# Layer borders of a seven-layer block: next layer's weights held early, its first products in a written order

## The chip, the cores and the metric

The kernel runs on one core of a Trainium2 chip. The metric is the device time of one execution in microseconds (us); several executions are timed and the median is given. The profile is of one further execution.

## The reference

One sequence of 512 tokens with 1024 features passes through two blocks. The first has a state-space mixer and a sliding-window attention, each between an RMS norm of its input and an RMS norm of its output:

```
for i in range(DEPTH):                       # mamba, then swa
    h = rmsnorm(x, pre_norm[i])
    y = mixer_i(h, ...)                      # ends in  o @ w_out
    x = x + rmsnorm(y, post_norm[i])
```

The second puts 16 meta tokens in front (528 tokens), and has a differential attention (da), a convolutional feed-forward (ffn0), a sparse attention with an index that picks keys (dsa), a second feed-forward (ffn1) and a final norm:

```
for i in range(DEPTH):                       # da, ffn0, dsa, ffn1
    h = h + attention_i(rms_norm(h, norm_i), w_in ...) @ w_o
    h = h + conv_ffn(rms_norm(h, ffn_norm[i]), w_up ...)   # u = h @ w_up first
```

A layer border is the stretch between the last product of one layer (`@ w_out`) and the first of the next (`h @ w_in`). At the borders mamba to swa and swa to da two norms lie in it, that of y and that of the new x.

## The kernel before

The features lie on the partitions, the tokens along the free axis; x is eight tiles `x[k]`. Every product is made in three terms to keep float32 accuracy: weights are split into `wH` and `wL`, the input into `hH` and `hL`, and for each of eight feature blocks k TensorE takes hH·wH, hH·wL and hL·wH (`gemm`, lines 353 to 368, and `project_v`, 785 to 805). `hH` comes from ScalarE (`high_of_x`, line 396), `hL` from VectorE (`low_of_x`, line 401). The norm's factor is not in h: it is multiplied into the product's result.

Weights arrive in chunks of eight 128x128 blocks: one load on SP's queue into `raw` (line 308), one ScalarE copy to `wH` (321), one VectorE subtraction to `wL` (323). `wH` and `wL` have a ring of four places each. `wget` has the chunk after the one asked for made as well.

A planner orders each engine's instructions when the program is built: of those that are ready by its own costs it takes the one that stands first in the program; a tile's place is given anew when its readers are done. The engines then run these fixed lists.

`norm_end` (line 459) makes the factor of the next norm: TensorE sums the squares over partitions (`token_sums`, 438), VectorE and GpSimd make the inverse root (`rsqrt`, 416 to 420: one GpSimd power, four small VectorE steps, the result is `rt`), TensorE spreads it over the partitions (`spread_rows`, 451 and 456), VectorE copies it to `rb` (468). `post_stats` does the same for the norm of y; its factor is `pr`.

`out_halves` (line 516 on) ends mamba and swa. For half 0 of the tokens, then half 1, it makes the eight output products of 12 matmuls, adds each to y (534) and collects squares (386 and 387). `post_update` then makes x = xs + y·factor (499, 500), `hH` and `hL` for one half. The order in the program is: half 0's products and factor; half 1's products; `post_update(0)`; two weight chunks (`W2 = 2`); half 1's factor; half 0's `post_norm` (squares, `norm_end`); `post_update(1)`; `post_norm(1)`. All four chunks of output weights lie in the ring.

swa begins with the keys (two products per half, then `rope`, lines 769 to 779) and the values (two tiles per half, line 797, brought out by ScalarE at 805 with `rt`). da begins with the values of five token tiles (16, 128, 128 in half 0; 128, 128 in half 1) for two groups of 256 columns. The other borders have no second norm: da and dsa end in `out_last`, ffn0 ends in its own loop, each with `norm_end(T)` as its last call, and ffn begins with `u = h @ w_up` in two column blocks per part. Results of these products go to five PSUM banks in turn (three `ps_g`, two `ps_s`).

Of the kernel before, what the change touches and what calls it, by code (L numbers as in the profile page):

```python
# [36 lines left out]
W1 = 0  # L37
W2 = 2
W3 = 0
# [176 lines left out]
class _Kernel:  # L216
# [225 lines left out]
    def spread_rows(self, src, T, half=None):  # L442
# [4 lines left out]
        for i, t0, tn in self.tok_tiles(T, half):  # L447
# [6 lines left out]
            if ps is None:  # L454
                ps, b0, n = self.ps("t"), t0, 0
# [4 lines left out]
    def norm_end(self, T, half=None):  # L460

        nc = self.nc
# [3 lines left out]
        self.rsqrt(self.rt[:, i0:i0 + n], v)  # L466
        for ps, t0, tn in self.spread_rows(self.rt, T, half):
            nc.vector.tensor_copy(self.rb[:, t0:t0 + tn], ps)

    def post_stats(self, half, acc, rg=None):  # L470
# [18 lines left out]
        return self.spread_rows(r, SEQ, half)[0][0]  # L489
# [17 lines left out]
    def post_norm(self, half, g_next, T_next):  # L507
# [3 lines left out]
        if g_next:  # L511
# [3 lines left out]
            self.norm_end(T_next, half)  # L515

    def out_halves(self, pool, H, L, ys, xs, g_post, g_next, T_next, acc, rg=None, part=True):
# [3 lines left out]
        n = len(H)  # L521

        for i in range(self.wi // 8, self.wi // 8 + n):
# [3 lines left out]
        ws = [self.wblocks(n) for m in range(KB)]  # L527
        rp = []
        for half in range(2):
            for m in range(KB):  # L530
                (ps, c0, cn), = self.gemm(ws[m], H, L, self.cuts(SEQ, half=half), spread=True)
                y = ys[m][:, c0:c0 + cn]
                if part:
                    nc.vector.tensor_tensor(y, ps, y, ALU.add)
                else:
                    nc.vector.tensor_copy(y, ps)
                self.square_in(y, m, c0, cn, nc.vector if m == KB - 1 else None, acc)
            if half == 1:
                for i in range(W1):
                    self.wchunk()  # L540
                self.post_update(0, rp[0], ys, xs, g_post, g_next, T_next)
                for i in range(W2):
                    self.wchunk()
            rp.append(self.post_stats(half, acc, rg))
        self.post_norm(0, g_next, T_next)
        for i in range(W3):
            self.wchunk()
        self.post_update(1, rp[1], ys, xs, g_post, g_next, T_next)
        self.post_norm(1, g_next, T_next)


    def mamba(self, g_next):
        nc, T = self.nc, SEQ
        tc = self.tc
        with ExitStack() as ctx:
# [210 lines left out]
            self.out_halves(op, yH[MF:], yL[MF:], yo, xo, "post0", g_next, SEQ, acc, rg)  # L766
# [17 lines left out]
    def project_v(self, vs, q, w, tiles, spread=False, meta=None):  # L784
# [3 lines left out]
        for i, t0, tn in tiles:  # L788
# [9 lines left out]
            qc = slice(256 * q, 256 * q + 256)  # L798
            if i == 0 and meta is not None:
                for r in range(2):  # L800
                    rv = lambda t: t.rearrange("p (b r n) -> p b r n", b=2, r=2)[:, :, r]
                    nc.scalar.activation(rv(meta[64 * r:64 * r + tn, qc]), rv(ps[:tn, :256]), AF.Copy,
                                         scale=self.rt[:tn, i:i + 1])
                continue
            nc.scalar.activation(vs[i][:tn, qc], ps[:tn, :256], AF.Copy, scale=self.rt[:tn, i:i + 1])
# [36 lines left out]

    def swa(self, g_next):
# [3 lines left out]
        with ExitStack() as ctx:  # L847
# [16 lines left out]
            kw = [self.wblocks(KB) for b in range(2)]  # L864
            vw = self.vweights()
            for half in range(2):
                cc = slice(256 * half, 256 * half + 256)
                nc.vector.tensor_tensor(C[:, cc], C[:, cc], self.rb[:, cc], ALU.mult)
                nc.vector.tensor_tensor(S[:, cc], S[:, cc], self.rb[:, cc], ALU.mult)
                for b in range(2):  # L870
                    self.rope(wp, self.gemm(kw[b], self.hH, self.hL, self.cuts(T, half=half), spread=True,
                                            late=True), C, S, kr[b])
                self.project_v(vs, 0, vw, self.tok_tiles(T, half), spread=True)
# [79 lines left out]
            if SF:  # L953
                for m in range(KB):
# [5 lines left out]
                            [x[:, META:] for x in self.x], "post1", g_next, T2, S, part=SF > 0)  # L960
# [129 lines left out]

    def da(self, g_next):
        nc, T = self.nc, T2
        with ExitStack() as ctx:
            cp = self.pool(ctx, "dc", 1, reuse_waits="tile")
# [23 lines left out]
            vw = [self.vweights() for q in range(2)]  # L1118
            for half in range(2):
                for q in range(2):  # L1120
                    self.project_v(vs, q, vw[q], self.tok_tiles(T, half), spread=True)
                for c0, cn in self.cuts(T, half=half):
                    nc.vector.tensor_tensor(C[:, c0:c0 + cn], C[:, c0:c0 + cn], self.rb[:, c0:c0 + cn], ALU.mult)
                    nc.vector.tensor_tensor(S[:, c0:c0 + cn], S[:, c0:c0 + cn], self.rb[:, c0:c0 + cn], ALU.mult)
# [143 lines left out]
    def out_last(self, H, L, g_next, lo=0):  # L1268
# [7 lines left out]
        if g_next:  # L1276
            self.norm_end(T)

# [213 lines left out]
    def ffn(self, i, g_next):  # L1492
# [6 lines left out]
        with ExitStack() as ctx:  # L1499
# [4 lines left out]
            for pi, part in enumerate(parts):  # L1504
                AH, AL = [], []
                for j in part:
                    cs = []
                    for s in range(2):
# [91 lines left out]
```

## Time and profile before

| | us |
|---|---|
| median of 3 runs | 2164.0 (2163.92 to 2164.73) |
| the profiled execution, its time | 2165.13 |
| its span, first to last instruction | 2162.7 |
| TensorE busy | 2076.2 (96%) |
| VectorE busy | 1488.3 (69%) |
| ScalarE busy | 1023.6 (47%) |
| GpSimd busy | 275.5 (13%) |
| granted TensorE clock, mean share of full | 0.981 |

The span is what the trace covers; the profiled execution's own time is 2.4 us more. Busy shares are means over all stages. In a timeline row the columns are start, duration, engine, line, operation, output and inputs, shape and count, and in brackets the idle time before it with what ended it.

### The profile page before, as it was taken

The numbers are of one execution on the slowest core, as the hardware profiler recorded it, in microseconds if no ns is written. First come the engines' busy times: TensorE is split into PE (matmuls) and PEld (weight loads), VectorE is DVE, ScalarE is ACT, GpSimd is POOL, SyncE is SP. The second block draws the span as 40 slices with busy tenths as digits, with TensorE's granted clock in tenths as the row PEclk, the third lists the DMA queues.
The fourth block names the chain that finished last, engine by engine and source line by source line (L and its number), as shares of the span: only waits on it lengthen the run. The fifth ranks groups of instructions, "written<-read, shape, count | busy, mean of one in ns | idle before, by whom it ended". The sixth has DMA issues, their size and how long they took to land. (4 is left out here: it accounts for less than half of the span.)

```text
span 2162.7 us, 37624 instructions
## 1 busy us (share of the span) xinstructions
PE 2076.2 (96%) x14812; PEld 1894.4 (88%) x14812; DVE 1488.3 (69%) x3215; ACT 1023.6 (47%) x1874; POOL 275.5 (13%) x433
## 2 busy tenths in 40 slices
PE   8999999989998899889999999989999999999998
PEld 6788888877777898879999999979888899999997
DVE  7786777787766666866763576489888667645653
ACT  6876555246675455644442343353455444423431
POOL 0211011141103222212000000210211020000001
PEclk9999999989999999989999999999999999999999
DMA  5333342413212222222332332311322222323221
GB/s 189 117 119 118 95 124 88 134 50 98 69 59 69 70 70 69 71 59 69 93 94 79 98 91 86 108 50 50 99 60 70 60 69 89 98 88 99 88 89 49
DMA packets 59567, 186.11 MB, mean 86 GB/s; under 512 B 8384, under 2 KB 12480, under 8 KB 59392
## 3 DMA queue, kind: packets, MB, share of 16 engines
q1 hardware_dynamic: 58240, 182.68, 28.2%
q8 instruction: 116, 1.90, 0.4%
q10 hardware_dynamic: 1152, 1.05, 0.1%
q14 instruction: 59, 0.48, 0.1%
HBM read 171.77 MB, written 2.23 MB: 80 GB/s over the span
## 5 line engine op out<-in xcount | busy, mean ns | idle before, releaser
L367 PE MATMUL ps_g<-hL,wH 128*128 128x256 f32 (+3 forms) x1912 | 606.7, 318 | 2.5 <-DVE hL L401 2.4
L367 PE MATMUL ps_g<-hH,wH 128*128 128x256 f32 (+3 forms) x1912 | 607.1, 318 | 1.4 <-ACT kr L775 1.1
L367 PE MATMUL ps_g<-hH,wL 128*128 128x256 f32 (+3 forms) x1912 | 606.5, 317 | 1.8 <-DVE wL L323 1.8
L321 ACT ACTIVATE wH<-raw 128x1024 fp32r<-128x1024 f32 x294 | 310.0, 1057 | 376.2 <-PE ps_g L367 217.1
L323 DVE TENSOR_TENSOR wL<-raw,wH 128x1024 fp32r<-128x1024 f32 x294 | 363.2, 1237 | 169.7 <-ACT wH L321 169.1
L367 PEld LDWEIGHTS ps_g<-hL,wH 128*128 128x128 f32 x1912 | 361.4, 189 | 26.9 <-DVE hL L401 3.9
L367 PEld LDWEIGHTS ps_g<-hH,wL 128*128 128x128 f32 x1912 | 362.3, 189 | 25.1 <-DVE wL L323 2.4
L367 PEld LDWEIGHTS ps_g<-hH,wH 128*128 128x128 f32 x1912 | 362.0, 189 | 24.1 <-ACT kr L775 1.2
L367 PE MATMUL ps_s<-hH,wH 128*128 128x256 f32 (+5 forms) x608 | 177.6, 292 | 8.0 <-ACT hH L396 8.0
L367 PE MATMUL ps_s<-hH,wL 128*128 128x256 f32 (+5 forms) x608 | 177.4, 292 | 0.6 <-DVE wL L323 0.6
L367 PE MATMUL ps_s<-hL,wH 128*128 128x256 f32 (+5 forms) x608 | 176.9, 294 | 0.7 <-DVE hL L401 0.6
L387 POOL TENSOR_TENSOR acc<-acc,sq 128x512 f32<-128x512 f32 (+3 forms) x62 | 78.1, 1260 | 555.5 <-ACT sq L386 554.1
L1519 DVE SCALAR_TENSOR_TENSOR c<-u,prm,c 128x528 f32<-128x528 f32 (+1 forms) x176 | 132.9, 755 | 1.6
L778 POOL TENSOR_TENSOR rt<-rt,S 128x272 f32<-128x272 f32 (+3 forms) x80 | 81.8, 1023 | 363.3 <-DVE rt L776 288.0
L367 PEld LDWEIGHTS ps_s<-hH,wH 128*128 128x128 f32 (+2 forms) x608 | 114.8, 189 | 10.4 <-ACT hH L396 9.1
L367 PE MATMUL ps_g<-aH,wH 128*128 128x256 f32 (+1 forms) x418 | 118.3, 283 | 0.3 <-ACT aH L810 0.2
L367 PEld LDWEIGHTS ps_s<-hL,wH 128*128 128x128 f32 (+2 forms) x608 | 114.3, 189 | 4.8 <-DVE hL L401 3.7
L367 PE MATMUL ps_g<-aL,wH 128*128 128x256 f32 (+1 forms) x418 | 118.2, 283 | 0.0
L367 PE MATMUL ps_g<-aH,wL 128*128 128x256 f32 (+1 forms) x418 | 118.0, 282 | 0.0
L367 PEld LDWEIGHTS ps_s<-hH,wL 128*128 128x128 f32 (+2 forms) x608 | 115.1, 189 | 3.3 <-DVE wL L323 1.4
L999 PE MATMUL ps_s<-k,q 128*128 128x272 f32 (+3 forms) x400 | 91.1, 323 | 13.6 <-DVE q L979 4.4
L810 ACT ACTIVATE aH<-sg 128x528 fp32r<-128x528 f32 (+1 forms) x44 | 28.1, 639 | 131.0 <-DVE sg L1524 131.0
(527 smaller groups left out, 4446.6 us busy)
## 6 DMA issues: line engine op xcount, KB each, us to landing
raw<-in_ws_dram SPq DMA_DIRECT2D x294, 512.0 KB, 3.7
k<-k SPq DMA_DIRECT2D x32, 264.0 KB, 3.1
m<-acs_d SPq DMA_DIRECT2D x32, 256.0 KB, 3.7
e<-eas_d SPq DMA_DIRECT2D x32, 96.0 KB, 2.8
x<-in_xT_dram SPq DMA_DIRECT2D x8, 256.0 KB, 4.9
xo<-in_xT_dram SPq DMA_DIRECT2D x8, 256.0 KB, 5.1
k<-k SPq DMA_DIRECT2D x4, 256.0 KB, 6.8
out_dram<-x SPq DMA_DIRECT2D x8, 128.0 KB, 1.7
```

The source lines that it names most:

```text
L321: nc.scalar.activation(H, self.raw, AF.Copy)
L323: nc.vector.tensor_tensor(L, self.raw, H.bitcast(F32), ALU.subtract)
L367: nc.tensor.matmul(ps[:M, :cn], w[k][a][:, :M], b[k][:, c0:c0 + cn], start=i == 0, stop=i == 3 * n - 1)
L387: (eng or nc.gpsimd).tensor_tensor(acc, acc, s[:, :cn], ALU.add)
L778: nc.gpsimd.tensor_tensor(t, t, S[:, cc], ALU.mult)
L810: nc.scalar.activation(H[:, cols], src, AF.Copy)
L999: nc.tensor.matmul(ps, q[:, r, t0:e], k[:, r, k0:k1], start=n == 0, stop=n == 1)
L1519: nc.vector.scalar_tensor_tensor(c[:, lo:], u[:, t + lo:t + T2], self.col(fw, 3 * b + t), c[:, lo:], ALU.mult, ALU.add)
```

## The change

- `out_halves`: of the four chunks of output weights two go to the ring and two to places of their own in the pool passed in. The chunks of the next layer follow in the ring: one after the fourth product of half 0 (if not yet made), one after the second and one after the fourth product of half 1. `W1`, `W2`, `W3` are gone.
- The factor of y's norm is made in two steps, `post_stats` and `post_spread`; the spread goes to the bank `ps_o`. `norm_end` is split into `norm_sums` and `norm_spread`.
- `front` is new. It takes up to four results ("banks"), and TensorE runs its part in the order written: for two banks at a time all products with hH, k by k; then `norm_sums`; then the products with hL for all banks, k by k; then `norm_spread`. Calls can be hung in after a given k.
- At the end of mamba and swa `front` is called for half 0 of the next layer. After the fourth k half 1's `post_stats` is hung in, after the twelfth (the fourth of the second pair) its `post_spread`. Then come `post_update(1)` and `post_norm(1)`, now without `norm_end`. The next layer calls `front` for half 1 (no calls hung in).
- `ahead(0)` gives what the next layer does with half 0's results (bringing out, tables, rope) a place in the program's order ahead of `post_update(1)`.
- da takes four of its six value products of half 0 in `front`, the two of the 16 tokens after it. Its pool `dc` is put on the right side of the memory.
- ffn0 and ffn1 take the first two parts' four column blocks in `front`; `norm_end` at the end of da and dsa is gone. The one at the end of ffn0 moves to the beginning of `dsa_index`, behind dsa's tables and memsets.

The diff, cut to its core:

```diff
-W1 = 0
-W2 = 2
-W3 = 0
...
     def norm_end(self, T, half=None):
+        self.norm_sums(T, half)
+        self.norm_spread(T, half)
...
+    def bank(self, w, c0, cn, M=P):
+        ps = self.ps(self.next_tag())[:M, :cn]
+        cc = slice(c0, c0 + cn)
+        return (ps, [[(w[k][a][:, :M], self.hH[k][:, cc]) for a in (0, 1)] for k in range(KB)],
+                [(w[k][0][:, :M], self.hL[k][:, cc]) for k in range(KB)])
...
+    def front(self, banks, T, half=None, hooks={}):
+        mm = self.nc.tensor.matmul
+        with self.tc.manual_schedule(engines={mybir.EngineType.PE}):
+            for b in range(0, len(banks), 2):
+                for k in range(KB):
+                    for ps, hs, ls in banks[b:b + 2]:
+                        for a, (w, h) in enumerate(hs[k]):
+                            mm(ps, w, h, start=k == 0 and a == 0, stop=False)
+                    hooks.get(KB * b // 2 + k, lambda: None)()
+            self.norm_sums(T, half)
+            for k in range(KB):
+                for ps, hs, ls in banks:
+                    w, h = ls[k]
+                    mm(ps, w, h, start=False, stop=k == KB - 1)
+            self.norm_spread(T, half)
+        return [b[0] for b in banks]
...
-        return self.spread_rows(r, SEQ, half)[0][0]
+        return r
+
+    def post_spread(self, r, half):
+        return self.spread_rows(r, SEQ, half, "o")[0][0]
...
-            self.norm_end(T_next, half)
...
+        c = self.wi // 8
+        for i in range(c, c + 4):
             if i >= self.wemit:
-                late = i - self.wi // 8 - 4
-                self.wchunk(*((pool, str(late)) if late >= 0 else ()))
+                self.wchunk(*((pool, str(i - c)) if i >= c + 2 else ()))
+        ws = [self.wblocks(4) for m in range(KB)]
...
+        for m in range(KB):
+            add(m, 0)
+            if m == 3 and self.wemit < c + 6:
+                self.wchunk()
+        rp = [self.post_spread(self.post_stats(0, acc, rg), 0)]
+        for m in range(KB):
+            add(m, 1)
+            if m in (1, 3):
+                self.wchunk()
+        second = []
+        self.post_update(0, rp[0], ys, xs, g_post, g_next, T_next)
         self.post_norm(0, g_next, T_next)
+        self.first = self.front(nxt(0), T_next, 0, {3: lambda: second.append(self.post_stats(1, acc, rg)),
+                                                    11: lambda: rp.append(self.post_spread(second[0], 1))})
+        self.prio = self.tc.cur_priority
         self.post_update(1, rp[1], ys, xs, g_post, g_next, T_next)
         self.post_norm(1, g_next, T_next)
+
+    def ahead(self, half):
+        tc = self.tc
+        return tc.high_priority(offset=tc.cur_priority - self.prio) if half == 0 else ExitStack()
...
+    def swa_first(self, half):
+        if half == 0:
+            self.fw = [self.wblocks(KB) for b in range(2)], self.vweights()
+        kw, vw = self.fw
+        return ([self.bank(w, 256 * half, 256) for w in kw] +
+                [self.bank_v(vw, t0, tn) for i, t0, tn in self.tok_tiles(SEQ, half)])
...
+                with self.ahead(half):
+                    ps = self.first if half == 0 else self.front(self.swa_first(1), T, 1)
+                    for (i, t0, tn), p in zip(tiles, ps[2:]):
+                        self.keep_v(vs, 0, i, tn, p)
...
+    def da_jobs(self, half):
+        t = self.tok_tiles(T2, half)[::-1]
+        return [(q, t) for ts in (t[:2], t[2:]) for q in range(2) for t in ts]
...
-            cp = self.pool(ctx, "dc", 1, reuse_waits="tile")
+            cp = self.pool(ctx, "dc", 1, reuse_waits="tile", side="right")
...
+                with self.ahead(half):
+                    ps = self.first if half == 0 else self.front(self.da_first(1), T, 1)
+                    for (q, (i, t0, tn)), p in zip(jobs, ps):
+                        self.keep_v(vs, q, i, tn, p)
+                    for q, t in jobs[4:]:
+                        self.project_v(vs, q, self.fw[q], [t], spread=True)
...
-        if g_next:
-            self.norm_end(T)
...
     def dsa_index(self, ip, C, S, sel):
         nc, T = self.nc, T2
+        self.norm_end(T)
...
+                    if j == 0:
+                        cuts = self.cuts(T, ulo)
+                        ps = self.front([self.bank(w, c0, cn) for w in [self.wblocks(KB) for s in range(2)]
+                                         for c0, cn in cuts], T)
...
-            if g_next and not final:
-                self.norm_end(T)
```

## Rows read from the trace of the kernel before

**Rows 1.** The page's first part: busy time, share of the span, instructions.

```profile
PE 2076.2 (96%) x14812; PEld 1894.4 (88%) x14812; DVE 1488.3 (69%) x3215; ACT 1023.6 (47%) x1874; POOL 275.5 (13%) x433
```

**Rows 2.** Longest wait of TensorE, 683 to 735 us: total us, times, longest.

```profile
PE ps_s L797 <- DVE wL L323: 5.2, 1, 5.2
```

**Rows 3.** Stretches: length; busy of each engine (instructions); granted clock, DMA, GB/s.

```profile
437.00:449.00 12.00, 11.53 (x96) 11.14 (x94) 9.71 (x28) 7.56 (x16) 5.30 (x7) 1.00 0.16 45
449.00:492.00 43.00, 36.45 (x222) 32.04 (x221) 36.84 (x87) 17.76 (x41) 18.11 (x24) 0.84 0.15 50
...
684.00:734.00 50.00, 38.79 (x268) 35.83 (x267) 31.56 (x74) 18.11 (x42) 15.92 (x25) 0.83 0.17 54
```

**Rows 4.** Stretches at half clock, same columns.

```profile
1775.00:1780.00 5.00, 5.00 (x32) 5.00 (x32) 2.43 (x4) 1.96 (x3) 0.00 (x0) 0.70 0.00 0
458.00:468.00 10.00, 9.45 (x60) 9.15 (x59) 6.45 (x19) 0.82 (x2) 2.48 (x2) 0.71 0.48 157
...
694.00:703.00 9.00, 9.00 (x58) 8.04 (x56) 4.95 (x17) 0.82 (x2) 1.80 (x2) 0.70 0.71 235
```

**Rows 5.** Timeline of TensorE, border mamba to swa.

```profile
449.36 0.28 PE L367 MATMUL ps_g<-hH,wH 128*128 128x256 f32 x1
...
451.60 0.57 PE L438 MATMUL ps_t<-ones,accy 128*128 128x1 f32 x4
...
491.77 0.40 PE L367 MATMUL ps_g<-hH,wH 128*128 128x512 f32 x1
```

**Rows 6.** Timeline of VectorE, border mamba to swa.

```profile
441.15 1.22 DVE L323 TENSOR_TENSOR wL<-raw,wH 128x1024 fp32r<-128x1024 f32 x1 [0.30 <-ACT wH L321]
...
451.70 6.15 DVE L401 SCALAR_TENSOR_TENSOR hL<-x,prm,hH 128x256 fp32r<-128x256 f32 x8
...
460.05 0.14 DVE L485 TENSOR_TENSOR nv<-ps_t,r 128x2 f32<-128x2 f32 x1
...
463.12 0.16 DVE L488 TENSOR_TENSOR pr<-pr,rg 128x2 f32<-128x2 f32 x1
465.50 0.48 DVE L499 SCALAR_TENSOR_TENSOR x<-x,prm,ps_t 128x256 f32<-128x256 f32 x1 [2.22 <-PE ps_t L456]
...
474.06 4.33 DVE L401 SCALAR_TENSOR_TENSOR hL<-x,prm,hH 128x256 fp32r<-128x256 f32 x8
```

**Rows 7.** Timeline of GpSimd, border mamba to swa.

```profile
452.10 5.07 POOL L387 TENSOR_TENSOR acc<-acc,sq 128x256 f32<-128x256 f32 x6 [1.81 <-ACT sq L386]
```

**Rows 8.** Timeline of TensorE, border swa to da.

```profile
683.79 0.28 PE L797 MATMUL ps_s<-wH,hH 128*16 128x256 f32 x1
...
693.60 0.40 PE L797 MATMUL ps_s<-wL,hH 128*16 128x256 f32 x1 [5.18 <-DVE wL L323]
...
734.12 0.28 PE L367 MATMUL ps_g<-hH,wH 128*128 128x272 f32 x1
```

**Rows 9.** Timeline of VectorE, border swa to da.

```profile
686.34 5.51 DVE L401 SCALAR_TENSOR_TENSOR hL<-x,prm,hH 128x272 fp32r<-128x272 f32 x7
...
694.61 0.15 DVE L479 TENSOR_SCALAR nv<-ps_t 128x2 f32<-128x2 f32 x1
...
697.30 0.16 DVE L420 TENSOR_TENSOR pr<-rs_r,rs_t 128x2 f32<-128x2 f32 x1
...
700.02 0.48 DVE L499 SCALAR_TENSOR_TENSOR k<-k,prm,ps_t 128x256 f32<-128x256 f32 x1 [2.56 <-PE ps_t L456]
...
709.67 3.79 DVE L401 SCALAR_TENSOR_TENSOR hL<-x,prm,hH 128x256 fp32r<-128x256 f32 x7
```

**Rows 10.** Timeline of ScalarE, border swa to da: a value tile brought out.

```profile
710.68 0.46 ACT L805 ACTIVATE v<-ps_g,rt 128x256 f32<-128x256 f32 x1
```

**Rows 11.** Timeline of TensorE, factor spread at ffn0's and ffn1's start.

```profile
1016.09 0.36 PE L451 MATMUL ps_t<-ident,rt 16*128 16x16 f32 x2 [1.12 <-DVE rt L420]
...
1774.17 0.39 PE L451 MATMUL ps_t<-ident,rt 16*128 16x16 f32 x2 [1.04 <-DVE rt L420]
```

**Rows 12.** Waits of TensorE over the whole span, its longest sum.

```profile
PE ps_t L1084 <- DVE p L1162: 9.9, 12, 1.2
```

More of the change, by code (lines that the diff above doesn't have):

```diff
@@ L440, in token_sums, with spread_rows @@
         return ps[:, i0:i0 + n], i0, n
-    def spread_rows(self, src, T, half=None):
+    def spread_rows(self, src, T, half=None, tag="t"):
         nc = self.nc
@@ L514, in post_norm, with out_halves @@
                                nc.vector if k == KB - 1 else None)
-            self.norm_end(T_next, half)
-    def out_halves(self, pool, H, L, ys, xs, g_post, g_next, T_next, acc, rg=None, part=True):
+    def out_halves(self, pool, H, L, ys, xs, g_post, g_next, T_next, acc, nxt, rg=None):
         nc = self.nc
-        n = len(H)
-        for i in range(self.wi // 8, self.wi // 8 + n):
+        c = self.wi // 8
+        for i in range(c, c + 4):
             if i >= self.wemit:
-                late = i - self.wi // 8 - 4
-                self.wchunk(*((pool, str(late)) if late >= 0 else ()))
[L527 to L544, printed above, removed]
@@ L797, in project_v, with keep_v @@
                 nc.tensor.matmul(ps[:tn, :256], a[k][:, t0:t0 + tn], w[k][b], start=n == 0, stop=n == 3 * KB - 1)
[L798 to L805, printed above, removed]
+            self.keep_v(vs, q, i, tn, ps[:tn, :256], meta)
+    def keep_v(self, vs, q, i, tn, ps, meta=None):
+        nc = self.nc
+        qc = slice(256 * q, 256 * q + 256)
+        if i or meta is None:
+            nc.scalar.activation(vs[i][:tn, qc], ps, AF.Copy, scale=self.rt[:tn, i:i + 1])
+            return
+        for r in range(2):
+            rv = lambda t: t.rearrange("p (b r n) -> p b r n", b=2, r=2)[:, :, r]
+            nc.scalar.activation(rv(meta[64 * r:64 * r + tn, qc]), rv(ps), AF.Copy, scale=self.rt[:tn, i:i + 1])
     def split(self, H, L, src, cols, gain=None):
@@ L863, in swa @@
             vs = [cp.tile([P, 256], F32, name=f"v{i}") for i in range(4)]
-            kw = [self.wblocks(KB) for b in range(2)]
-            vw = self.vweights()
             for half in range(2):
                 cc = slice(256 * half, 256 * half + 256)
[L868 to L873, printed above, removed]
+                tiles = self.tok_tiles(T, half)
+                with self.ahead(half):
+                    ps = self.first if half == 0 else self.front(self.swa_first(1), T, 1)
+                    for (i, t0, tn), p in zip(tiles, ps[2:]):
+                        self.keep_v(vs, 0, i, tn, p)
+                    nc.vector.tensor_tensor(C[:, cc], C[:, cc], self.rb[:, cc], ALU.mult)
+                    nc.vector.tensor_tensor(S[:, cc], S[:, cc], self.rb[:, cc], ALU.mult)
+                    for b in range(2):
+                        self.rope(wp, [(ps[b], 256 * half, 256)], C, S, kr[b])
             k2 = [self.stack(cp, kr[b], f"k2{b}") for b in range(2)]
@@ L1089, in turns_of, with da_first @@
         return [t[:, P * j:P * j + P] for j in range(len(srcs))]
+    def da_jobs(self, half):
+        t = self.tok_tiles(T2, half)[::-1]
+        return [(q, t) for ts in (t[:2], t[2:]) for q in range(2) for t in ts]
+    def da_first(self, half):
+        if half == 0:
+            self.fw = [self.vweights() for q in range(2)]
+        return [self.bank_v(self.fw[q], t0, tn) for q, (i, t0, tn) in self.da_jobs(half)[:4]]
     def da(self, g_next):
@@ L1117, in da @@
             nc.gpsimd.memset(vs[0], 0.0)
-            vw = [self.vweights() for q in range(2)]
             for half in range(2):
[L1120 to L1124, printed above, removed]
+                jobs = self.da_jobs(half)
+                with self.ahead(half):
[4 more added lines that the diff above has]
+                        self.project_v(vs, q, self.fw[q], [t], spread=True)
+                    for c0, cn in self.cuts(T, half=half):
+                        cc = slice(c0, c0 + cn)
+                        nc.vector.tensor_tensor(C[:, cc], C[:, cc], self.rb[:, cc], ALU.mult)
+                        nc.vector.tensor_tensor(S[:, cc], S[:, cc], self.rb[:, cc], ALU.mult)
             OH = [cp.tile([P, T2], F32R, name=f"o{h}H") for h in range(8)]
```

29 lines of the change are left out of this document (22 added, 7 removed).

## Prediction

> **What bounds the kernel now.** I read the page's first part, then the waits of TensorE, then stretches around the borders, then the timelines of single engines in them. TensorE is busy for 96% of the span [rows 1], so over most of it only fewer or faster matmuls would help. What the change can win is where TensorE is not fed. In an undisturbed stretch of output products 96 instructions take 11.53 us, 0.12 us each [rows 3]. From the first product of swa to the first after its keys and values, 449.36 to 491.77 [rows 5], pass 42.4 us; they hold 192 products (two keys and two value tiles of 24 matmuls, for two halves), which at 0.12 us are 23.0. The border to da runs from 683.79 to 734.12 [rows 8], 50.3 us, with 240 products (ten value tiles), 28.8. So some 19.4 and 21.5 us are lost at these two borders, in which the granted clock is 0.84 and 0.83 [rows 3]. Part of this is the clock itself: after TensorE was starved it stands at 0.71 and 0.70 of full for 10 and 9 us [rows 4], some 6 us at 1.2 GHz and the rest at 2.4.
>
> What ends the waits is VectorE. At border one it is busy 36.84 of 43 us [rows 3]: eight hL in 6.15 us, then conversions of weights, and only then the small steps of half 1's factor, 460.05 to 463.28 [rows 6]. At border two the longest wait, 5.2 us, is for a wL [rows 2] that stands behind seven hL of 5.51 us [rows 9].
>
> **Border mamba to swa.** Of what VectorE does, nothing goes: four conversions of 1.22 us [rows 6] stay four. Two now fall before or into half 0 and two into half 1's products, where one was; so what follows on VectorE comes 1.2 us later. I start where half 1's products end, at 449.36.
> Sixteen products, 1.9 us, to 451.3. Then the sums of y, which in the trace run at 451.60 for 0.57 [rows 5]: 452.1. The next 32 products, 3.8 us, to 455.9. Now TensorE's written order has the spread of half 1's factor, and nothing behind it may pass. The factor needs VectorE, which by the program's order first does the eight hL: 451.70 + 1.2 + 6.15 = 459.1. The chain from the first small step to the last took 3.2 us here and 2.85 at the next border [rows 6, 9], both with work between; I take 2.85, since one conversion no longer stands in it: 462.0. TensorE stands 6.1 us. After it come the spread, 0.4, 48 products, 5.8, sums and spread of the next norm, 0.9; and as it was starved I charge the fall of the clock that followed such a wait before [rows 4], with about 5 us of work at half speed, 2.5: 471.6. Half 1's hH come 8.6 us after its factor (465.50 to 474.06, where the hL begin [rows 6]): 462.4 + 8.6 = 471.0, so half 1's 96 products, 11.5, and 0.9 for sums and spread run through to 484.0. Its hL (4.33 us) lie beside them.
> The next weights are a new cost. Before, the keys' chunks came free one by one; now hL of all banks is last, so chunks come free from the middle of the last 32 products on. A copy, a subtraction of 1.22 [rows 6] and their start come to some 2.7 us against 1.9 left: 0.8 us. Bounds 0 (the planner gives the earliest place) and 2.7. End: 484.8 against 491.77, 7.0 us won.
>
> **Border swa to da.** The two chunks in the pool's own places can be made only when the last head's buffers are free. The trace shows no such wait; its bounds are 0 and the two subtractions, 2.4; I take 1.0, as the third chunk is wanted only at the fifth of eight products: start 684.8. Sixteen products and the sums of y as above, 2.6, to 687.4; 32 products to 691.2. The factor: seven hL end at 691.85 [rows 9], 1.2 later is 693.1, and 2.85 more 695.9; TensorE stands 4.7. Spread 0.4, 48 products 5.8, sums and the wider spread 1.2, half clock 2.5: 705.8. The two products of the 16 tokens, 48 matmuls, 5.8: 711.6. Half 1's hH are there 9.7 us after the factor (700.02 to 709.67 [rows 9]), at 706. So 12.4 us for half 1, 724.0, and 0.8 for the weights: 724.8 against 734.12, 9.3 us won.
> The value tiles must leave their banks for this. Before, the first left at 710.68 [rows 10], when half 1's hL had begun [rows 9]; that it waited for memory that swa still used is a guess. The pool on the right side should end that; if not, up to 5 us come back (711 against 706).
>
> A rule of the Trainium skill bears on the stand of 6.1 us. The row shows eight hL in 6.15 us beside 5.07 us of GpSimd's adds [rows 7], and 4.33 for those of half 1 [rows 6]. The page "SBUF — State Buffer", section "SBUF: two separate sides", says that VectorE with two SBUF inputs and GpSimd take an exclusive lock on a shared port, and the loser stands for the whole instruction. Full blocking would make up to 4.33 + 5.07 = 9.4 us of the first eight; the trace does not bear that out, it shows 1.8 us of slowing. By the rule both stands would be up to 3.2 us longer and the result 2151; I keep the measured 6.15.
>
> **The other borders.** In ffn0 and ffn1 the factor's spread stood before the third column block: 1.12 and 1.04 us idle [rows 11]. In `front` 64 products lie between x and the sums and 32, 3.8 us, between sums and spread, so both waits go. After the second the clock fell: 32 products in 5.00 us [rows 4] are 1.2 over 32 at 0.12. Together 3.3 us. The results leave later and four at once; the fifth bank covers that, as a product lasts 2.9 us. Border ffn0 to dsa keeps its norm, now placed behind dsa's memsets; I count nothing, with bounds of 1.2 either way, about the wait at the like places [rows 11].
>
> **Sum.** 7.0 + 9.3 + 3.3 = 19.6 us. The profiled execution took 2165.1 (span 2162.7), so 2145.5; the median of the runs lies 1.1 below it: 2144.
>
> **Rivals.**
> *The spread does not stand.* If the planner's list for VectorE has half 1's small steps between the hL, TensorE never starves and the clock stays. Border one is then held by half 1's hH, at 471.5 for the last, and ends with 3.8 + 0.9 + 3.8 + 0.8 at about 481; border two at 691.2 + 0.4 + 5.8 + 1.2 + 5.8 + 12.4 + 0.8 = 717.6. That wins 3.5 and 7.2 more: 2134. Against it: in the trace the small steps come after all hL [rows 6, 9].
> *VectorE is the border.* At border one its idle time is 43 − 36.84 = 6.2 us [rows 3] and some of it is latency; if only half can go, 3.1 is won; at border two 4.3 if the value tiles leave late again (9.3 − 5); with about 2 at the ffn: 2155. For it speaks the busy share, against it that the tables and ropes may come behind TensorE's border.
> *The early work holds the update back.* `ahead` puts half 0's tables and rope ahead of `post_update(1)`. If VectorE's list does so too, x of half 1 begins 9 us later at border one (471.6, not 462.4) and at border two 10 (706, not 695.9), and TensorE starves once more with another fall of the clock: nearly all is given back, 2163.
> *Slower: new lists in the attentions.* The planner makes all lists anew, and the shift at the borders changes what is ready when. In da TensorE waits 12 times for p, 9.9 us in all and at most 1.2 [rows 12]. If each of 24 heads in the three attentions got one more wait of the longest kind, 28.8 us, the result would be 2174; it decides from 0.8 us a head on, where 19.6 is used up. Against it: nothing of the attentions is edited.
>
> **How the numbers follow.** Forecast 0.50 (by itself 2136 to 2152, from the bounds of weights, places and chain), no stand 0.15, VectorE 0.17, update held back 0.08, slower lists 0.10. A measurement of this kernel can tell about 0.2%, 4.3 us, from no change. Faster holds the first two and most of the third, 0.80; no change the fourth and the edges, 0.11; slower 0.09. The range goes from 2129, below the no-stand case, to 2162: beyond it are the slower lists, part of the held-back case and a little below, less than 0.2.
>
> **What would show it.** Right: in both borders TensorE's longest wait is before the spread in the twelfth k, for VectorE's small step, 4 to 6 us, with the clock at half after it; half 1's `front` runs without a gap over 1 us; the borders take 35 and 41 us. Wrong: no gap there (the first rival), gaps in half 1's products with hH (the third), or the borders shorter and heads of an attention longer (the fourth). The forecast is wrong altogether if the span between the borders' ends does not keep its length.

## The result and the profile after

The changed kernel takes 2153.43 us (median of 5 runs, 2149.52 to 2157.01) against 2164.73 of the kernel before (2163.92 to 2165.77): ratio 0.9949, 95% interval 0.9936 to 0.9962. It is 11.3 us faster, by a little over half of the 19.6 that were forecast. The profiled execution is its fastest (2149.52, span 2147.5), so the difference of the two first traces, 15.2 us of span, is larger than that of the medians. To tell chance from change, the table has a second trace of each kernel and, from the experiments, one with the feed-forward part alone and one with the two large borders alone. Each number is the distance between two starts in a timeline of TensorE; a border reaches from the first product of the next layer to the first one behind its written part, as the 42.4 and 50.3 us of the prediction.

| trace | start to border 1 | border 1 | rest of swa | border 2 | from there to the end |
|---|---|---|---|---|---|
| before | 449.4 | 42.4 | 192.0 | 50.3 | 1428.6 |
| before, again | 447.7 | 42.3 | 192.1 | 50.3 | 1431.3 |
| feed-forward part alone | 449.4 | 42.9 | 192.1 | 50.5 | 1425.4 |
| changed | 446.2 | 40.3 | 195.7 | 42.3 | 1423.1 |
| changed, again | 446.1 | 41.8 | 195.8 | 40.8 | 1425.5 |
| two borders alone | 446.7 | 41.8 | 195.9 | 40.5 | 1432.5 |

Means of three against three: border 1 wins 1.2 us (forecast 7.0), the rest of swa loses 3.7 (forecast none), border 2 wins 9.2 (forecast 9.3), the feed-forward part wins 6.1 behind border 2 (forecast 3.3). The first column differs by 2.5 us; in the traces this arises at about 60 us, in code that the change doesn't touch. Border 1 and the rest of swa together lose 2.5 us, where the forecast had them win 7.0.

The page's first part of the changed kernel, which answers to [rows 1]; with as many instructions, TensorE is busy for 12.0 us less:

```profile
PE 2064.2 (96%) x14812; PEld 1885.1 (88%) x14812; DVE 1487.0 (69%) x3215; ACT 1023.3 (48%) x1874; POOL 277.8 (13%) x433
```

The waits of TensorE in the changed kernel, 440 to 495 us (us in total, times, longest):

```profile
PE ps_g L502 <- ACT v L856: 4.1, 1, 4.1
PE ps_o L453 <- DVE pr L530: 3.5, 1, 3.5
PE ps_t L453 <- DVE rt L417: 3.4, 1, 3.4
PE ps_g L502 <- ACT hH L393: 1.2, 1, 1.2
```

The second is the stand that was forecast, at 6.1. The first and the third were not. The same for 675 to 730 us, where the wait of 5.2 for wL [rows 2] is gone:

```profile
PE ps_s L849 <- ACT v L856: 2.3, 1, 2.3
PE ps_o L453 <- DVE pr L417: 2.2, 1, 2.2
PE ps_s L502 <- ACT hH L393: 1.3, 2, 1.2
```

TensorE's timeline at border 1 (answers to [rows 5]): first product, spread of half 1's factor, the second bank of half 1, last spread, first product behind the border:

```profile
446.20 0.28 PE L502 MATMUL ps_g<-hH,wH 128*128 128x256 f32 x1
...
457.82 0.68 PE L453 MATMUL ps_o<-ident,pr 128*128 128x128 f32 x4 [3.54 <-DVE pr L530]
...
469.37 0.39 PE L502 MATMUL ps_g<-hH,wH 128*128 128x256 f32 x1 [4.09 <-ACT v L856]
...
486.05 0.68 PE L453 MATMUL ps_t<-ident,rt 128*128 128x128 f32 x4 [3.37 <-DVE rt L417]
486.49 0.54 PE L364 MATMUL ps_g<-hH,wH 128*128 128x512 f32 x1
```

Why the bank comes late stands in ScalarE's timeline of the changed kernel. Half 0's products were done at 464.6, but a value tile leaves at 468.87, behind the hH and the squares of half 1, which wait for its x:

```profile
464.17 0.91 ACT L393 ACTIVATE hH<-x,prm 128x256 fp32r<-128x256 f32 x2 [2.07 <-DVE x L546]
464.99 0.71 ACT L383 ACTIVATE sq<-x 128x256 f32<-128x256 f32 x2
...
468.54 0.42 ACT L383 ACTIVATE sq<-x 128x256 f32<-128x256 f32 x1
468.87 0.82 ACT L856 ACTIVATE v<-ps_g,rt 128x256 f32<-128x256 f32 x2
```

Why the last spread is late stands in VectorE's. The sums were done at 478.8; half 1's first small step comes at 484.18, behind the rotation tables (from 472.18) and half 0's rope (from 481.12):

```profile
472.18 0.42 DVE L880 CAST ang<-posi 128x512 f32<-128x512 int32 x1
...
481.12 0.45 DVE L828 STREAM_SHUFFLE rt<-kr 128x256 f32<-128x256 f32 x1
...
483.51 0.75 DVE L831 TENSOR_TENSOR kr<-kr,rt 128x256 f32<-128x256 f32 x2
484.18 0.15 DVE L466 TENSOR_SCALAR nv<-ps_t 128x2 f32<-128x2 f32 x1
...
485.74 0.16 DVE L417 TENSOR_TENSOR rt<-rs_r,rs_t 128x2 f32<-128x2 f32 x1
```

At border 2 there is a stand that TensorE doesn't show. VectorE waits 2.07 us for the sums of half 0's next norm, whose first step stands in its list ahead of most of half 1's x, and 0.74 more for GpSimd's power. At border 1, where the clock had not fallen at this place, the same wait for the sums is 0.28 in this trace; here the clock stands at 0.50 from 695 to 698 us:

```profile
698.66 0.16 DVE L466 TENSOR_SCALAR nv<-ps_t 128x3 f32<-128x3 f32 x1 [2.07 <-PE ps_t L435]
698.74 0.41 DVE L546 TENSOR_TENSOR x<-x,k 128x256 f32<-128x256 f32 x1
699.89 0.69 DVE L414 TENSOR_TENSOR rs_t<-nv,rs_r 128x3 f32<-128x3 f32 x1 [0.74 <-POOL rs_r L413]
```

Stretches of the changed kernel (length, busy time of each engine, granted clock, DMA; [rows 3, 4] of before):

```profile
446.00:486.50 40.50, 28.15 (x221) 27.22 (x219) 35.60 (x88) 15.91 (x39) 15.90 (x21) 0.96 0.02 9
...
486.50:490.50 4.00, 3.92 (x13) 2.86 (x12) 4.00 (x11) 3.44 (x5) 1.63 (x2) 0.57 0.45 133
682.00:724.50 42.50, 36.61 (x273) 33.16 (x272) 27.64 (x73) 16.83 (x41) 16.73 (x24) 0.92 0.04 15
...
1766.00:1771.00 5.00, 5.00 (x43) 4.82 (x42) 4.73 (x9) 2.25 (x4) 0.00 (x0) 1.00 0.37 110
```

The second row is part of what swa loses. The stand before the last spread is followed by 4 us at a clock of 0.57, (1 − 0.57) × 4 = 1.7 us, now behind the border. 1.0 more is a wait for wL at the first output product that needs a chunk in the pool's own places: two products of one bank start 1.13 us apart in place of 0.12. The remaining 1.0 lies just ahead of it, in the same output products: 17 starts from 659.59 to 663.59 take 4.00 us, where 0.12 each makes 2.0. Of this, 0.3 is a wait for an oH at 660.17; the rest I have not resolved.

```profile
662.46 0.39 PE L364 MATMUL ps_g<-oH,wH 128*128 128x256 f32 x1
663.59 0.39 PE L364 MATMUL ps_g<-oH,wL 128*128 128x256 f32 x1 [0.75 <-DVE wL L320]
```

### The profile page after: what moved, and what is told of

Its sections match the earlier page's. It is cut to its first block, busy times and chain, and to the rows that moved or that the text cites. A ratio compares the mean times of both kernels' runs of the same rounds, so it can differ in the third digit from the quotient of the medians.

```text
span 2147.5 us, 37629 instructions
## 1 busy us (share of the span) xinstructions
PE 2064.2 (96%) x14812; PEld 1885.1 (88%) x14812; DVE 1487.0 (69%) x3215; ACT 1023.3 (48%) x1874; POOL 277.8 (13%) x433
## 4 chain that ended last, share of the span: by engine, by line
PE 77%; DVE 11%; ACT 6%; issue 3%; POOL 1%; DMA 1%; SPq 0%; POOLq 0%; DVEq 0%; ACTq 0%
PE ps_g L364 48%; PE ps_s L364 14%; DVE wL L320 2%; PE ps_s L1062 2%; PE ps_o L1448 1%; PE ps_t L1147 1%; PE ps_g L849 1%; DVE sel L1558 1%; PE ps_o L1248 1%; DVE m L1557 1%; PE ps_s L766 1%; ACT wH L318 1%; PE ps_o L1001 1%; ACT q L1041 1%; PE ps_g L502 1%
## 5 line engine op out<-in xcount | busy, mean ns | idle before, releaser
L364 PE MATMUL ps_g<-hH,wL 128*128 128x256 f32 (+3 forms) x1856 | 590.4, 318 | 2.1 <-DVE wL L320 2.0
L364 PE MATMUL ps_g<-hH,wH 128*128 128x256 f32 (+3 forms) x1856 | 590.6, 318 | 0.0
L364 PE MATMUL ps_g<-hL,wH 128*128 128x256 f32 (+3 forms) x1856 | 590.3, 318 | 0.0
L364 PEld LDWEIGHTS ps_g<-hH,wL 128*128 128x128 f32 x1856 | 350.6, 189 | 26.0 <-DVE wL L320 3.5
L364 PEld LDWEIGHTS ps_g<-hL,wH 128*128 128x128 f32 x1856 | 350.4, 189 | 23.0 <-issue 2.9
L364 PEld LDWEIGHTS ps_g<-hH,wH 128*128 128x128 f32 x1856 | 350.4, 189 | 22.7 <-issue 1.0
L364 PE MATMUL ps_s<-hH,wH 128*128 128x256 f32 (+5 forms) x568 | 165.1, 291 | 6.6 <-ACT hH L393 6.6
L364 PE MATMUL ps_s<-hH,wL 128*128 128x256 f32 (+5 forms) x568 | 164.7, 290 | 0.0
L364 PE MATMUL ps_s<-hL,wH 128*128 128x256 f32 (+5 forms) x568 | 164.7, 290 | 0.0
L364 PEld LDWEIGHTS ps_s<-hH,wL 128*128 128x128 f32 (+2 forms) x568 | 106.3, 187 | 2.5 <-issue 1.0
```

The lines of the kernel that those rows point to most:

```text
L364: nc.tensor.matmul(ps[:M, :cn], w[k][a][:, :M], b[k][:, c0:c0 + cn], start=i == 0, stop=i == 3 * n - 1)
```

## The experiments

The theory on which they rest: border 1 fell short because two engines carry fixed lists in which work for half 1 and work with half 0's results stand in the wrong order. Its main rival is the prediction's second, that VectorE's work is the bound, so that a stand taken away comes back elsewhere. The experiments ran in three groups, each with the kernel before timed beside it (medians 2163.7, 2164.6 and 2164.5 us); ratios are to that one.

**Both kernels again.**

> The changed kernel itself once more, as the measure for the runs beside it. Theory (the lists fall short of the forecast in fixed places): the two borders come out as in the first trace, 40.3 and 42.3 us from the first product of a layer to the first after its written part, with stands of TensorE of 3.5, 4.1 and 3.4 us at the first border and 2.3 twice at the second; time 2150 to 2157. Rival (chance in the first trace): the borders differ by over 1 us and the stands fall in other places. The 3 us by which the first trace was ahead before 62 us, in code that the change leaves alone, are chance by either: they may be absent here.

2152.26 us (2150.46 to 2153.89; ratio 0.9947, 0.9933 to 0.9960). The stand for the bank is 4.1 again, that before the last spread 3.3; the one for the factor 2.0 in place of 3.5, because the clock had already fallen before it (0.64 in 450 to 454 us, 1.00 in the first trace). Border 1 is 1.5 longer and border 2 is 1.5 shorter, with a stand for the value tile of 0.9 in place of 2.3; both are outside what was expected.

> The kernel before once more, for a second profile. Theory: the two borders come out as in its first trace, 42.4 and 50.3 us within 1 us. Open: in its first trace TensorE stood 2.0 us at 58 to 61 us for a DMA of mamba and the clock fell after it, in eight traces of kernels with the change it stood 0.5 to 1.7 and the clock did not fall. If that is chance, this trace lies somewhere between; if it hangs on the kernel, 2.0 again.

2164.50 us (ratio 1.0001, 0.9992 to 1.0011). Borders 42.3 and 50.3: they repeat within 0.1. At 58 to 61 us TensorE stood 1.6 us and the clock stayed at 1.00. The wait for that DMA (ScalarE's, 2.5 to 4.4 us over the traces) differs from run to run. That the first column of the table is chance altogether is not shown: the three traces with the old borders lie at 447.7 to 449.4, the eleven with the new ones at 446.1 to 447.8.

**The change in two parts.** The first kernel is the one before with the edits below (and `front` with the functions it needs), the second the changed one without them (and with `norm_end` back at the end of da, ffn0 and dsa).

```diff
+                    if j == 0:
+                        cuts = self.cuts(T, ulo)
+                        ps = self.front([self.bank(w, c0, cn) for w in [self.wblocks(KB) for s in range(2)]
+                                         for c0, cn in cuts], T)
...
-        if g_next:
-            self.norm_end(T)
```

> The kernel before with the two feed-forward borders of the change alone (first four column blocks in the written order, the factor within them). By the forecast's third term 3.3 us less, by the two traces 0.7 and 3.35: 2159.5 to 2161. Rival (the fall of the clock at the second of these borders is chance, and only the two waits of about 1 us go): 2 us less, 2161.5 to 2162.5.

2158.17 us (2156.96 to 2161.91; ratio 0.9971, 0.9961 to 0.9981): 6.5 us, more than either. Its trace in the table is of the slowest of its eight executions.

> The change without its feed-forward part: the borders into swa and da as in the changed kernel, those into ffn0, ffn1 and dsa as before. Theory (the feed-forward part alone gave 6.5 us in the runs, so the two large borders, forecast at 16.3, give what is left of 11.5): 5 us less than before, 2158 to 2160.5. Rival (the traces are right, where the feed-forward part gave 2.5 to 4, and the large borders 8 to 9): 2155 to 2157.

2157.46 us (2155.55 to 2160.04; ratio 0.9973, 0.9962 to 0.9983): 7.0 us, between the two. The ratios multiply to 0.9944, against 0.9949 and 0.9947 for the whole: the parts add up. So the two large borders, forecast at 16.3, gave about 7.

**Half 1's factor first on VectorE.** An edge of order, no wait, from the factor's last step to the second part of the tables (`late_tab`).

```diff
-        self.rsqrt(self.rt[:, i0:i0 + n], v)
+        self.last_rt = self.rsqrt(self.rt[:, i0:i0 + n], v)
...
+            self.chain(self.last_rt, self.late_tab)
```

> One edge of order on VectorE is added: in swa the factor of half 1 stands ahead of the second part of the rotation tables (and so of half 0's rope). Theory: the stand of 3.4 us before the last spread of the first border goes and nothing takes its place before the first scores; that of 4.1 us for a bank stays. First border 36.5 to 37, and 3.4 to 5.2 us less in all (the upper end if the fall of the clock behind the stand goes too): 2148 to 2150 beside a changed kernel at 2153. Rival (VectorE's work is the bound of the border): tables and rope come later by what the factor comes earlier, TensorE stands as long at the first scores, and the time is within 1 us of the changed kernel's.

2152.06 us (2150.90 to 2154.96; ratio 0.9946, 0.9933 to 0.9958): the rival's time. The stand before the spread is gone, border 1 takes 38.9, but the rest of swa 198.2, 2.4 us more than in the changed kernel. The waits of TensorE in this kernel, 486 to 500 us:

```profile
PE ps_g L364 <- DVE wL L320: 3.4, 2, 3.0
```

The tables, the rope and behind them the next weights came later by what the factor came earlier. Taking a stand away by order alone moved it.

**Half 0's banks first on ScalarE.** The list could not simply be changed. The planner treats a pool of tiles as one when it decides what is ready: swa's first pool lies over mamba's pool of squares, so whatever writes the former stands, in the list, behind the last square. That is why `ahead` had no effect; built without it, ScalarE's and VectorE's lists differ from the changed kernel's only in the place of two small instructions of da. So the squares' tiles were moved (mamba's to the other side, swa's ahead of its first pool), and ScalarE's order laid down by edges; h and s are hH and squares of half 1, out what empties half 0's banks.

```diff
-            self.squares(ctx)
+            self.squares(ctx, side="right")
...
+            self.squares(ctx)
             cp = self.pool(ctx, "sc", 1, reuse_waits="tile")
...
+        self.chain(h[0], h[1], s[0], s[1], h[2], s[2], out[0], h[3], h[4], *out[1:], s[3], h[5], s[4], h[6], s[5],
+                   h[7], s[6], s[7])
```

> ScalarE empties half 0's four banks (the first before the fourth of half 1's hH, the others before the sixth) in both borders; for this the tiles of squares of mamba and swa lie in memory that the next layer's first pool doesn't use. Theory (the results leave their banks late because ScalarE's list has all squares of half 1 ahead of them): the stands of 4.1 and 2.3 us go, half 1's products are held by its hH alone (last one near 469.5 and 707), first border 33 to 35, second 39 to 40.5, in all 2143 to 2147. If the factor of half 1 still stands behind the tables, the first border keeps 40 and only the second gains: 2150. Rival (half 1's hH and VectorE's work hold the border anyway): the stands move behind the later hH, both borders within 1 us of 40.3 and 42.3, time 2152 to 2154.

2147.87 us (2146.16 to 2151.80; ratio 0.9928, 0.9916 to 0.9941). The stands of 4.1 and 2.3 are gone, border 2 takes 38.5, a little less than expected; border 1 takes 37.1, 2 more than expected, with a stand of 2.0 before the last spread, and the rest of swa is 4.1 longer than in the changed kernel. So border 1 and swa together are no shorter (237.0 us, against 236.0 and 237.6 in the changed kernel's two traces and 237.1 in the run above); what is won in the traces lies at border 2.

> The changed kernel with the tiles of squares of mamba and swa in memory that the next layer's first pool doesn't use, and no order laid down for ScalarE. Theory (it is this memory that puts all squares of half 1 ahead of half 0's results in the planner's list): half 0's results leave ahead of the last hH and square, 1 us sooner, and the factor of half 1 comes ahead of the rope; first border 37 to 39, of which swa gives 2 to 3 back; second 40 to 42; in all 2149 to 2151.5. Rival (only the laid down order does it): as the changed kernel, 2152 to 2154.

This is the same without the edges. 2149.97 us (2146.58 to 2154.12; ratio 0.9940, 0.9928 to 0.9953). The median is 2.3 below the changed kernel's second one, which is within their spread. What the run shows is the order. The move alone puts half 0's value tiles ahead of half 1's last hH in ScalarE's list:

```profile
470.62 0.82 ACT L862 ACTIVATE v<-ps_g,rt 128x256 f32<-128x256 f32 x2
...
471.86 0.52 ACT L393 ACTIVATE hH<-x,prm 128x256 fp32r<-128x256 f32 x1
```

It also puts half 1's factor ahead of half 0's rope in VectorE's. The stand for a bank shrinks from 4.1 to 3.2 and the one before the last spread goes, but a wait of 3.0 for wL comes behind it: border 1 takes 36.1, swa 199.5. So it is the memory of the squares that held the order; the edges do the rest.

**The spread after the sixteenth k.**

```diff
-                                                    11: lambda: rp.append(self.post_spread(second[0], 1))})
+                                                    15: lambda: rp.append(self.post_spread(second[0], 1))})
```

> The changed kernel with the spread of half 1's factor after the sixteenth k in place of the twelfth, and nothing else. Theory (what is won ahead of the squares is given back, as long as ScalarE empties half 0's banks behind all squares of half 1): the stand for a bank grows by what the stand for the factor loses; first border 39.5 to 41, second 40 to 41.5, total at most 2 us below the changed kernel: 2150 to 2153. Rival (the later spread brings the next norm's sums and so x of half 1 forward by itself, as between the two runs with the banks first, 2147.9 and 2143.1): borders 3.7 and 2.8 us shorter, 2145 to 2148.

2148.79 us (2145.30 to 2153.18; ratio 0.9924, 0.9910 to 0.9938). In the trace it went as the theory has it: the stand for the factor shrinks to 1.7, the one for the bank grows to 4.5 and at border 2 to 3.0, the borders take 40.1 and 42.1. `rt` does come sooner, 15.2 us behind the border's first product in place of 17.9, but the value tiles still leave behind half 1's last hH. The median is below the expected range, its interval reaches into it; the trace is of the slowest of the six executions, and the median lies nearer to the rival's 2145 to 2148. The run does not decide between them.

> As the run before, and the spread of half 1's factor hangs after the sixteenth k in place of the twelfth, so that 16 more products lie beside the wait for the factor. Theory: the stand of 3.5 us shrinks by 1.9 at each border, but half 1's x, hH and so the end of the border hang on the factor itself, which comes no sooner: within 1 us of the run before. Rival (the forecast's sum: everything behind the spread comes 1.9 earlier): 1.9 less at each border, 3.8 in all; and with no fall of the clock behind a stand of 1.6 up to 3 us more.

With the banks first, 2143.11 us (2137.35 to 2146.71; ratio 0.9898, 0.9883 to 0.9914): my theory was wrong, borders 33.4 and 35.7 are 3.7 and 2.8 shorter. VectorE shows why. With the spread after the twelfth k, its timeline:

```profile
463.77 0.16 DVE L468 TENSOR_SCALAR nv<-ps_t 128x2 f32<-128x2 f32 x1 [2.12 <-PE ps_t L437]
...
467.28 0.35 DVE L419 TENSOR_TENSOR rt<-rs_r,rs_t 128x2 f32<-128x2 f32 x1
```

and after the sixteenth:

```profile
460.50 0.15 DVE L468 TENSOR_SCALAR nv<-ps_t 128x2 f32<-128x2 f32 x1
...
462.96 0.15 DVE L419 TENSOR_TENSOR rt<-rs_r,rs_t 128x2 f32<-128x2 f32 x1
```

All products with hH now lie before the stand, so the sums of half 0's next norm follow at once, VectorE does not stand for them ahead of half 1's x, and `rt`, which the banks need, comes 15.2 us behind the border's first product in place of 20.4. About half of this is the clock: in the changed kernel's first trace, with the spread after the twelfth k and the clock at 1.00 at this place, `rt` comes after 17.9. In the trace of this run the clock stays at 1.00 through both borders; in the other, which is of the slowest of its five executions, it is 0.91 and 0.96. So the 6.5 us by which the borders differ are too much. Executions of the two kernels with the same mean clock (0.988 and 0.989) are some 3 us apart: 2144.5 and 2143.1 here, 2147.6 and 2146.2 with the spread after the twelfth k.

**Tables early.** This asks whether VectorE's work is the bound: some 7 us of it leave the border for mamba's last products, where VectorE is busy for 9.9 of 20 us (420 to 440 us in the changed kernel).

```diff
             wctx.close()
+            self.tabs = ExitStack()
+            tp = self.pool(self.tabs, "tb", 1, reuse_waits="tile", side="right")
...
+                self.swa_tables(self.pool(tctx, "st", 1, reuse_waits="tile", side="right"), self.C1, self.S1)
```

> The changed kernel with swa's rotation tables (about 7 us of VectorE) made in mamba's last products, where VectorE is half idle, in place of the border; nothing else. Theory (VectorE's work is the bound at the end of the first border and at the start of swa, so that putting the factor first only moved the stand): the stand of 3.4 before the last spread goes and is not given back in swa; first border 36.5 to 38.5, from its end to swa's end 195.7 or less, in all 2147 to 2149.5. Rival (the give-back of 2.5 us in swa came from the order of the weights, not from VectorE's load): first border shorter by 3.4, swa longer by 2 to 4, time 2151 to 2153. A third way: the tables delay the end of mamba by up to 2 us.

2154.66 us (2151.31 to 2155.99; ratio 0.9948, 0.9934 to 0.9961): none of the three. At the place asked about, the theory is right: border 1 takes 38.4 and the rest of swa 195.8, so nothing is given back. But border 2 takes 46.1. There TensorE stands 5.9 us for a value tile, and ScalarE, with its list unchanged, shows what it waits for:

```profile
705.72 0.42 ACT L383 ACTIVATE sq<-x 128x256 f32<-128x256 f32 x1
709.65 0.47 ACT L868 ACTIVATE v<-ps_s,rt 128x256 f32<-128x256 f32 x1 [3.51 <-DVE acc L384]
```

swa's first pool had shrunk by the tables, its squares had moved down, and da's first value tile lay on the last of them.

```diff
             C, S = self.C1, self.S1
+            pad = cp.tile([P, 2 * T], F32, name="pad")
+            nc.gpsimd.memset(pad[:, :1], 0.0)
```

> As the run with the early tables alone, and 4 KB of unused memory a partition in swa's first pool, so that swa's squares lie where they lay in the changed kernel and not under da's first value tiles. No instruction changes but one memset of one column. Theory (there da's first value tile waited 3.5 us for the last add of the squares, whose memory it got): the stand of 5.9 for a bank at the second border goes back to 2.3, the border from 46.1 to 41 to 42.3, in all 2149.5 to 2152 against 2154.7. Rival (the longer border came from the lists): 46 again and 2154 to 2156.

2149.54 us (2145.50 to 2151.26; ratio 0.9934, 0.9922 to 0.9946): 4 KB of unused memory a partition is worth 5 us. Border 2 is back at 40.7, and TensorE's wait there, 675 to 730 us, at that of the changed kernel:

```profile
PE ps_s L861 <- ACT v L868: 2.3, 1, 2.3
```

**All of it**: banks first, spread after the sixteenth k, tables early, the squares of swa at the bottom of its memory, and no `ahead`.

> Banks first, the spread after the sixteenth k, and the tables made in mamba's last products. Theory (the three act in different places and add up): first border 31 to 33, from its end to swa's end 195 to 197, second border 35.5 to 36, 2137 to 2141. Rival (what is left is latency, not VectorE's load): as with the first two alone, 2142 to 2145.

2137.51 us (2135.41 to 2138.58; ratio 0.9872, 0.9858 to 0.9886), 27 us faster than the kernel before and the best version here. Border 1 takes 31.4, the rest of swa 194.7, border 2 37.1 (1 more than expected). The waits of TensorE, 440 to 500 us:

```profile
PE ps_o L455 <- DVE pr L532: 1.7, 1, 1.7
PE ps_s L985 <- DVE q L1064: 1.4, 1, 1.4
PE ps_g L504 <- ACT hH L394: 1.2, 1, 1.2
PE ps_s L504 <- ACT hH L394: 0.8, 1, 0.8
PE ps_g L504 <- ACT v L878: 0.4, 1, 0.4
```

ScalarE now frees a bank at 464.11, and half 1's hH end with that of 468.74, 21.7 us behind the border's first product (21.8 in the changed kernel):

```profile
464.11 0.45 ACT L878 ACTIVATE v<-ps_g,rt 128x256 f32<-128x256 f32 x1
464.47 0.90 ACT L394 ACTIVATE hH<-x,prm 128x256 fp32r<-128x256 f32 x2
...
468.74 0.49 ACT L394 ACTIVATE hH<-x,prm 128x256 fp32r<-128x256 f32 x1
```

## Why the prediction was right, and where its sizes were off

- *Direction and range* held: 2153.4 lies between 2129 and 2162, 9.4 above the 2144. It is 1.4 above the 2136 to 2152 that the sum's own bounds gave. That the sum came no further off is in part luck: border 1 with swa fell short by 9.5, the feed-forward part won more than its term, and the first column of the table, in no term, may have helped.
- *Border 1* is the term that was mis-sized: 7.0 forecast, 1.2 won and more than that lost behind it. The failed step is "half 1's `front` runs without a gap over 1 us" and "so half 1's 96 products, 11.5, and 0.9 for sums and spread run through to 484.0". Two stands lie in it, 4.1 for a bank and 3.4 for the last spread. The step counted when half 1's hH come, and that was about right (last one at 468.0, forecast 471.0 for a start 3.2 later). It did not ask when half 0's banks are emptied, although five banks serve eight products, nor what else stands in VectorE's list ahead of half 1's factor.
- *The stand in the twelfth k* is there, for VectorE's small step, as said, but it is 3.5 and 2.0 us, not 6.1, and 2.2 to 2.3, not 4.7. The hL began 3.4 us behind the border's first product, as forecast (3.5). They took 5.66 us, not 6.15 [rows 6]; the chain took 2.1 (455.56 to 457.67), not 2.85, with no other work in it; and 1.2 of the wait had been spent before, on hH: 0.5 + 0.75 + 1.2 of the 2.6 by which 6.1 was too long. By the rule of the Trainium skill ("SBUF — State Buffer", section "SBUF: two separate sides") the hL could have taken up to 9.4, the prediction's estimate; the 5.66 us, beside 4.54 us of GpSimd's adds, do not bear the rule's full blocking out. The result of 2151 that it gave is nearer to the measured one, but for another reason.
- *Border 2* came out as forecast in size, 9.2 against 9.3, but by luck: the 9.3 have in them the 1.0 for the pool's own places, which was paid inside swa, so the border itself was forecast to win 10.3; and the stand for the value tile (2.3) and VectorE's wait for the sums (2.07) took what the shorter stand in the twelfth k gave. Of "the pool on the right side should end that" nothing shows: built with that pool on the left, the lists are the same. That was not run.
- *The pool's own places* cost the 1.0 that was taken, but inside swa, beside 1.0 more in the same products that no term had.
- *The feed-forward part* was under-sized, 3.3 forecast, 6.1 to 6.5 measured. By the traces about 1.7 lie in the stretch with ffn0 and 3.7 in that with dsa and ffn1; the rest lies in da, which this part doesn't touch. Both waits are gone as said. The fall of the clock behind the second is gone too, but the second trace of the kernel before doesn't have it either (1.00 from 1775 to 1780 us behind the same wait of 1.0), so the 1.2 charged for it was not a sure gain. What else the clock gained in those stretches differs from trace to trace and I cannot assign it.
- *Rivals.* "VectorE is the border" named a place, 2155, 1.6 from the measured time, and the experiments bear part of it out. Border 1 and the rest of swa took 236.0 and 237.6 us in the changed kernel; the factor first or the banks first left that at 237.1 and 237.0, while VectorE's load taken away made it 234.2 and 232.8, the later spread with the banks first 231.6 (in a trace whose clock held at border 1), and all together 226.1. So two orders only moved the stand, but one gave as much as the load. "The early work holds the update back" was wrong in its cause, since `ahead` changes no list, but a relative of it is real: the early norm step holds half 1's x back, by 2.07 us where the clock had fallen and by 0.28 where it had not. "The spread does not stand" and "slower lists" are refuted; swa's loss is in two places, not in each head. In the prediction's sums for these two, the 3.5 won at border 1 should be 4.0 (484.8 less 480.8), and 2174 counts from 2145.5, not from 2144; neither changes the reading.

## What to carry to other kernels

For every result that is started early, write down which engine empties its bank and what stands ahead of that in the engine's list; a free input is worth nothing while the bank is full. A planner's list can be held by memory alone: look which earlier tiles the new pool lies on before reaching for priorities. A stand removed by order alone can come back on the engine that carries both pieces of work, as it did in three runs here; try to take the work away as well, and then read the whole layer, not the border.

## What the runs showed of the hardware that was not expected

The clock's falls do not follow the length of a stand in these traces. In the changed kernel's first trace a stand of 3.5 us for the factor left the granted clock at 1.00 for the next 8 us; in four other traces (factor first, banks first, tables early with and without padding) the same stand had a fall to 0.50 beside it or close behind it. In its second trace a stand of 1.2 for hH was followed by 0.64 in 450 to 454 us; in its first the same stand left the clock at 1.00.

The levels are 0.50 and 1.00 of 2.4 GHz. At the borders of the changed kernel most falls lasted some 3 to 4 us and one 7; elsewhere they were longer (0.52 over the 14 us from 936 to 950 in the second trace of the kernel before).

The spread of the runs goes with this: of the changed kernel's first five, over 7 us apart, the fastest (2149.52) has a mean granted clock of 0.988 and the slowest (2157.01) 0.984; the four of the version without long stands are 3 us apart, at 0.989 to 0.991. The first trace is of the fastest run, which is why one trace of each kernel put the gain at 15. That the falls cause most of the spread is likely but not shown.
